# The last projection of a hybrid encoder layer: ten token tiles in one group, seven block products per column pair

## The chip, the cores and the metric

The kernel runs on one core of one Trainium2 chip. The metric is the device time of one execution in microseconds. The kernel before took 2684.31 us in the median of three runs (2681.81 to 2684.42).

Names of the engines: PE is the tensor engine (PEld its weight loads), DVE the vector engine, ACT the scalar engine, POOL the GpSimd engine, SP the engine whose queue issues all DMAs of this kernel. SBUF is the working memory, PSUM the accumulators in eight banks of 512 columns each.

## The reference

One layer of an encoder with two kinds of heads, computed for 1024 and 256 tokens, in fp32:

```python
hn = rmsnorm(x, norm_w)
proj = jnp.einsum('btd,dp->btp', hn, w_in)
# group A: neighbourhood attention, times a SiLU gate       -> att, 1024 wide
# group B: bidirectional mLSTM, norm, two gates             -> mem, 1024 wide
mixed = jnp.concatenate([att, mem], axis=-1)
return x + jnp.einsum('btm,md->btd', mixed, w_out)
# and last: y = rmsnorm(y, final_norm_w)
```

The change touches only the last lines: a product of 1280 tokens by 2048 by 2048 columns, plus the residual `x`, and the norm of each row.

## The kernel before

All token counts are together 1280 = 10 tiles of 128. The layer runs in three stages. Stage A projects the first 768 tokens; it already uses seven block products for a 2x2 block matrix (lines 314 to 383). Then the remaining 512 tokens are projected in pairs of 128 columns (`proj_pair`, line 488), interleaved with attention and mLSTM, which leave their result in DRAM as 16 blocks `mixT[k]` of 128 features by 1280 tokens. At the end of that, `late_gate` (line 530) projects the gates of the last 512 tokens, multiplies them into `mixT` and stores it back: first for features 1024 to 2047 (line 1168), then for features 0 to 1023 (line 1182). Last comes the output projection.

Every fp32 matrix product is made of three passes. An operand is split into a high part (a cast to fp32r on ACT, line 151) and a low part (source minus high part, a subtraction on DVE, line 152); high x high, high x low and low x high are accumulated. A matmul of the last stage has a 128x128 piece of `mixT` as the stationary operand and 512 columns of the output weights as the moving one, so a bank holds 128 tokens by 512 columns.

The output projection before (lines 1171 to 1244) goes over three groups of token tiles, `OG`: four, four and two. For a group all 16 blocks of `mixT` are loaded and split into the buffers that held the inputs of the projections before (`x_pair`, line 137). For each of four column blocks of 512, eight weight pieces of 512 KB are loaded and split (`w_split`, line 477), and for each block `k` the tiles of the group are multiplied with it. The last four blocks are held until the end, and then run tile by tile, so that the banks are finished one after the other. Each finished bank is read by DVE, which adds the residual (line 1240), ACT squares the result and sums it (line 1241), and POOL multiplies it with the norm weight (line 1242). After the fourth column block `finish` (line 1189) takes the row's reciprocal root mean square and scales and stores the row.

The order on each engine is chosen when the kernel is built, by a scheduler that follows the program's order and the buffers; at run time each engine keeps to that order. All loads and stores go through the one queue of SP, in order.

Of the kernel before, what the change touches and what calls it, by code (L numbers as in the profile page):

```python
# [13 lines left out]
P = 128  # L14
D = 2048
# [23 lines left out]
def kernel(  # L39
# [26 lines left out]
    def bank(tag, name):  # L66
        return ps.tile([P, 512], F32, tag=tag, name=name, bufs=3 if tag == "pr" else 5)
# [398 lines left out]
    def po(name):  # L466
        return wb.tile([P, 520], F32, tag="po", name=name, bufs=NPO)
# [6 lines left out]
        DM.dma_start(dst, src)  # L474
        return raw

    def w_split(raw, lo_, hi_, name, keep=False):
        n = hi_ - lo_
        if keep:
            t = yp.tile([P, 2, 512], F32R, tag="wk", name=f"ws_{name}", bufs=4)  # L480
        else:
            t = wb.tile([P, 2, 544], F32R, tag="wsp", name=f"ws_{name}", bufs=4)
        split(t[:, 0, :n], t[:, 1, :n], raw[:, lo_:hi_])
        return t

# [637 lines left out]
        for J in range(nc_):  # L1123
            yield out_unit(J)

    ahead = {}

    class LazyX:
        def __init__(self):
            self.t = {}  # L1130
# [37 lines left out]
    for ch in range(0, 8, 2):  # L1168
        late_gate(OT0 + ch, 8 + ch, X)

    OG = ((0, 4), (4, 4), (8, 2))

    def mix_raw(g, k):
        t0, n = OG[g]
        raw = po(f"mraw{g}_{k}")[:, : n * P]
        DM.dma_start(raw, mixT[k][:, t0 * P : (t0 + n) * P])
        return raw

    for h in range(0, NA_H, 2):
        if h == NA_H - 2:  # L1180
            ahead = {k: mix_raw(0, k) for k in range(2)}
        late_gate(GT0 + h, h, X)
    att_ctx.close()

    yp = ctx.enter_context(tc.tile_pool(name="yp", bufs=2))
    fnb = yp.tile([P, D], F32, tag="fnb", name="fnb", bufs=1)
    DM.dma_start(fnb, fnw.partition_broadcast(P))

    def finish(t, yt, ss):
        rs = yp.tile([P, 1], F32, tag="rs", name=f"rs{t}", bufs=4)  # L1190
        V.tensor_reduce(rs, ss, axis=mybir.AxisListType.X, op=ALU.add)
        rsqrt_mean(rs, rs, 1, float(D))
        w_ = 512 if t == TT // P - 1 else 1024
        for i in range(D // w_):
            cs = slice(i * w_, i * w_ + w_)
            if i % 2:
                S.mul(yt[:, cs], yt[:, cs], rs)
            else:
                V.tensor_scalar(yt[:, cs], yt[:, cs], rs, None, op0=ALU.mult)
            DM.dma_start(y[t * P : (t + 1) * P, cs], yt[:, cs])  # L1200

    for g, (t0, n) in enumerate(OG):
        mh, ml_ = [None] * KT, [None] * KT
        for k in range(KT):
            raw = ahead[k] if g == 0 and k in ahead else mix_raw(g, k)
            mh[k], ml_[k] = x_pair(k, f"m{g}_{k}")
            split(mh[k][:, : n * P], ml_[k][:, : n * P], raw)
        yt = [yp.tile([P, D], F32, tag="y", name=f"y{g}_{t}", bufs=5) for t in range(n)]
        ss = [yp.tile([P, 4], F32, tag="ss", name=f"ss{g}_{t}", bufs=8) for t in range(n)]

        def out_mm(o, tt, k, t, first, last):
            for i, (wi, xi) in enumerate(((1, 0), (0, 0), (0, 1))[:: 1 if tt % 2 else -1]):
                PE.matmul(  # L1213
                    o, (mh[k], ml_[k])[xi][:, tt * P : (tt + 1) * P], t[:, wi, :512],
                    start=first and i == 0, stop=last and i == 2,
                )

        for nb in range(4):
            held = []
            n_hold = 8 if (g, nb) == (2, 3) else 4  # L1220
            banks = [bank("pr" if nb % 2 and i < 3 else "a", f"po{g}_{nb}_{i}") for i in range(n)]
            for kp in range(0, KT, 2):
                nm = f"o{g}_{nb}_{kp}"
                raw = yp.tile([P, 1024], F32, tag="wr", name=f"wr_{nm}", bufs=4)
                DM.dma_start(raw, w_o[nb, :, kp * 512 : kp * 512 + 1024])
                for q in range(2):
                    k = kp + q
                    t = w_split(raw, q * 512, q * 512 + 512, f"{nm}_{q}", KT - n_hold <= kp < KT - 4)
                    if kp >= KT - n_hold:
                        held.append((k, t))  # L1230
                        continue
                    for tt in range(n):
                        out_mm(banks[tt], tt, k, t, k == 0, False)
            for tt in range(n):
                for i, (k, t) in enumerate(held):
                    out_mm(banks[tt], tt, k, t, False, i == n_hold - 1)
                cs = slice(nb * 512, nb * 512 + 512)
                xr = yp.tile([P, 512], F32, tag="xr", name=f"xr{g}_{nb}_{tt}", bufs=4)
                DM.dma_start(xr, xtok[(t0 + tt) * P : (t0 + tt + 1) * P, cs])
                V.tensor_tensor(yt[tt][:, cs], banks[tt], xr, op=ALU.add)  # L1240
                S.activation(xr, yt[tt][:, cs], AF.Square, accum_out=ss[tt][:, nb : nb + 1])  # L1241
                G.tensor_tensor(yt[tt][:, cs], yt[tt][:, cs], fnb[:, cs], op=ALU.mult)  # L1242
                if nb == 3:
                    finish(t0 + tt, yt[tt], ss[tt])


def _layout(inputs):
# [84 lines left out]
```

## Time and profile before

| | |
|---|---|
| median of three runs | 2684.31 us |
| span of the profiled execution | 2680.8 us |
| PE, busy | 2631.7 us |
| DVE, busy | 1797.0 us |
| ACT, busy | 1307.0 us |
| POOL, busy | 617.9 us |
| read from and written to device memory | 322.28 and 66.13 MB |
| granted clock of PE, mean | 0.997 |

The profile is of one execution. Its span runs from the first to the last instruction; the time of a run also holds what lies around it. A row of the groups of instructions names the line, the engine, the operation, the tile written and the tiles read, shapes and count; behind the bar stand the busy time in us and the mean of one instruction in ns, and after the second bar how long the engine was idle ahead of these instructions and what ended the wait. Line 151 and 152 are helpers, so one looks at the tile's name: `ws_o` are split weights of the last projection, `m_` split mix blocks, `po` its banks.

### The profile page before, as it was taken

The numbers are of one execution on the slowest core, as the hardware profiler recorded it, in microseconds if no ns is written. First come the engines' busy times: TensorE is split into PE (matmuls) and PEld (weight loads), VectorE is DVE, ScalarE is ACT, GpSimd is POOL, SyncE is SP. The second block draws the span as 40 slices with busy tenths as digits, with TensorE's granted clock in tenths as the row PEclk, the third lists the DMA queues.
The fourth block names the chain that finished last, engine by engine and source line by source line (L and its number), as shares of the span: only waits on it lengthen the run. The fifth ranks groups of instructions, "written<-read, shape, count | busy, mean of one in ns | idle before, by whom it ended". The sixth has DMA issues, their size and how long they took to land.

```text
span 2680.8 us, 42790 instructions
## 1 busy us (share of the span) xinstructions
PE 2631.7 (98%) x14710; PEld 2407.5 (90%) x14710; DVE 1797.0 (67%) x3645; ACT 1307.0 (49%) x2995; POOL 617.9 (23%) x897
## 2 busy tenths in 40 slices
PE   8999999999999999999999999999999999999998
PEld 8899999999999999988888898998888888878876
DVE  7867878788877878773676677586577444353455
ACT  7534444444444444533665666665665223242344
POOL 0434445444444444200110110100010000020121
PEclk9999999999999999999999999999999999999999
DMA  6423333332323233535555555655654545354465
GB/s 207 154 73 124 109 112 114 103 95 95 107 77 113 95 100 97 177 111 162 168 176 172 188 167 169 209 163 170 207 158 148 189 141 198 112 197 152 135 222 171
DMA packets 206435, 391.24 MB, mean 146 GB/s; under 512 B 25952, under 2 KB 117256, under 8 KB 206088
## 3 DMA queue, kind: packets, MB, share of 16 engines
q1 hardware_dynamic: 206216, 388.49, 45.3%
q8 instruction: 116, 1.90, 0.3%
q14 instruction: 103, 0.84, 0.1%
HBM read 322.28 MB, written 66.13 MB: 145 GB/s over the span
## 4 chain that ended last, share of the span: by engine, by line
PE 51%; DMA 4%; DVE 3%; ACT 1%; issue 1%; SPq 0%; POOL 0%; ACTq 0%; POOLq 0%; DVEq 0%
PE pc L500 20%; PE po L1213 16%; PE pv L581 5%; PE A54b L188 1%; PE A52b L188 1%; DMA wr<-in_w_in_dram 1%; PE nap_0s L618 1%; PE nap_1s L618 1%; DMA nap_0vr<-vD 0%; DMA mlp_0zr<-pT 0%; DMA wr_o<-in_w_o_dram 0%; PE nap_1o L744 0%; PE nap_0t L635 0%; PE nap_1t L635 0%; PE nap_0o L744 0%
## 5 line engine op out<-in xcount | busy, mean ns | idle before, releaser
L152 DVE TENSOR_TENSOR ws_o<-wr_o,ws_o 128x512 fp32r<-128x512 f32 x192 | 148.2, 783 | 150.4 <-ACT ws_o L151 148.3
L152 DVE TENSOR_TENSOR ws<-wr,ws 128x512 fp32r<-128x512 f32 x224 | 153.2, 694 | 127.1 <-ACT ws L151 125.7
L151 ACT CAST ws<-wr 128x512 fp32r<-128x512 f32 x224 | 136.9, 619 | 176.1 <-PE pc L500 133.7
L151 ACT CAST ws_o<-wr_o 128x512 fp32r<-128x512 f32 x192 | 116.5, 618 | 173.4 <-PE po L1213 146.9
L1242 POOL TENSOR_TENSOR y<-y,fnb 128x512 f32<-128x512 f32 x40 | 58.1, 1463 | 538.1 <-ACT xr L1241 517.1
L1240 DVE TENSOR_TENSOR y<-po,xr 128x512 f32<-128x512 f32 x40 | 27.5, 689 | 51.0 <-PE po L1213 51.0
L1241 ACT ACTIVATE xr<-y 128x512 f32<-128x512 f32 x40 | 25.2, 629 | 65.6 <-DVE y L1240 65.6
L165 DVE TENSOR_TENSOR pco<-pc,rstdb 128x512 f32<-128x512 f32 x48 | 32.9, 687 | 35.7 <-PE pc L500 34.1
L152 DVE TENSOR_TENSOR wsv<-wr_v,wsv 128x512 fp32r<-128x512 f32 x64 | 44.0, 693 | 18.8 <-ACT wsv L151 15.3
L102 POOL TENSOR_SCALAR mls_0r<-mls_0r 128x2 f32<-128x2 f32 x4 | 1.2, 289 | 234.6 <-ACT mls_0jk L1090 234.6
L151 ACT CAST wsv<-wr_v 128x512 fp32r<-128x512 f32 x64 | 38.8, 616 | 31.6 <-PE pc L500 19.3
L274 DVE SCALAR_TENSOR_TENSOR pcv<-pco,cw_sb,pcv 128x516 f32<-128x516 f32 x64 | 46.6, 748 | 0.0
L500 PE MATMUL pc<-x_0h,ws 128*128 128x512 f32 x112 | 36.0, 401 | 0.9 <-DVE pco L165 0.9
L188 PE MATMUL fb<-xg,fw 128*128 128x384 f32 x192 | 35.1, 336 | 1.7 <-ACT xg L158 1.7
L500 PE MATMUL pc<-x_2h,ws 128*128 128x512 f32 x112 | 35.4, 399 | 0.0
L188 PEld LDWEIGHTS fb<-xg,fw 128*128 128x128 f32 x192 | 33.3, 188 | 2.2 <-ACT xg L158 2.2
L500 PE MATMUL pc<-x_8h,ws 128*128 128x512 f32 x112 | 34.6, 396 | 0.0
L500 PE MATMUL pc<-x_1h,ws 128*128 128x512 f32 x112 | 34.4, 395 | 0.0
L188 PE MATMUL fb<-xb,fw 128*128 128x384 f32 x96 | 23.2, 355 | 11.0 <-ACT xb L158 11.0
L500 PE MATMUL pc<-x_9h,ws 128*128 128x512 f32 x112 | 33.7, 397 | 0.0
L500 PE MATMUL pc<-x_5h,ws 128*128 128x512 f32 x112 | 33.1, 397 | 0.0
L500 PE MATMUL pc<-x_4h,ws 128*128 128x512 f32 x112 | 33.1, 397 | 0.0
(1734 smaller groups left out, 8767.0 us busy)
## 6 DMA issues: line engine op xcount, KB each, us to landing
wr<-in_w_in_dram SPq DMA_DIRECT2D x112, 512.0 KB
wr_o<-in_w_o_dram SPq DMA_DIRECT2D x96, 512.0 KB
wr_v<-in_w_in_dram SPq DMA_DIRECT2D x32, 512.0 KB
xq<-in_xtok_dram SPq DMA_DIRECT2D x20, 512.0 KB
xr<-in_xtok_dram SPq DMA_DIRECT2D x40, 256.0 KB
out_dram<-y SPq DMA_DIRECT2D x18, 512.0 KB
mraw<-mx SPq DMA_DIRECT2D x32, 256.0 KB
xr<-in_xT_dram SPq DMA_DIRECT2D x16, 384.0 KB
```

The lines of the kernel that those rows point to most:

```text
L151: S.copy(hi, src)
L152: V.tensor_tensor(lo, src, f(hi), op=ALU.subtract)
L165: V.tensor_tensor(o, src, rb, op=ALU.mult)
L188: PE.matmul(o, w(a_), x(b_), start=first and m == 0, stop=last and m == 2)
L274: V.scalar_tensor_tensor(dst[:, a:n], src[:, a + j - pad : n + j - pad], cw_sb[:, ct, j : j + 1], dst[:, a:n], op0=ALU.mult, op1=ALU.add,)
L500: PE.matmul(pb[j], t[j][:, wi, c : c + P], xs[xi], start=first and m == 0, stop=last and m == 2,)
L581: PE.matmul(outs[tt], xs[:, tt * P : (tt + 1) * P], t[:, wi, q * w : (q + 1) * w], start=first and m == 0 and (gates or tt % 2 == 0), stop ...
L618: PE.matmul(b[:, :nkeys], qs(a_), ks(b_), start=i == 0, stop=i == 2)
L1213: PE.matmul(o, (mh[k], ml_[k])[xi][:, tt * P : (tt + 1) * P], t[:, wi, :512], start=first and i == 0, stop=last and i == 2,)
L1240: V.tensor_tensor(yt[tt][:, cs], banks[tt], xr, op=ALU.add)
L1241: S.activation(xr, yt[tt][:, cs], AF.Square, accum_out=ss[tt][:, nb : nb + 1])
L1242: G.tensor_tensor(yt[tt][:, cs], yt[tt][:, cs], fnb[:, cs], op=ALU.mult)
```

## The change

The output projection is one group of all ten tiles. The mix matrix is cut into 2 x 2 blocks: features 0 to 1023 and 1024 to 2047 (`kh`), and tokens 0 to 639 and 640 to 1279 (`th`, five tiles each). In the code `a` and `d` are the blocks of the first tokens (low and high features), `e` and `c` those of the last tokens. The weights are taken for a pair `p` of two column blocks, again as 2 x 2 blocks (`b11`, `b12`, `b21`, `b22`). The four result blocks of a pair are then sums of seven products instead of eight. Written with the numbers of the code, in the order in which they run: product 2 = d x b21; 5 = (e + c) x (b12 - b11); 1 = a x b11; 6 = (e + c - a) x T2 with T2 = b22 - b12 + b11; 7 = (c - e') x (b22 - b12); 4 = c x (T2 - b21); 3 = (d - e') x b22, where e' is the block e after e + c - a was put in its place. For the second pair product 2 comes last, and is marked as the tail, whose blocks are all split ahead and which runs tile by tile.

A product has eight blocks `kk` of 128 features. For each, ACT and DVE split a mix piece of 128x640 into a buffer `mo` (four of them) and a weight piece of 128x512 into a buffer `wsp` (four). Sums of mix blocks are made by DVE, in place or in a buffer `ms` (two), sums of weight blocks by POOL. The last two blocks are held (`HOLD`), and then each tile's bank is finished and read.

The result blocks are accumulators `Y` in SBUF, in the buffers of the earlier inputs (`xslot`). They are loaded with the residual `xtok` (`y_init`), and each finished bank is added to one or two of them by DVE (`y_add`); the banks of products 1, 6 and 7 are the same, accumulated further. Finished blocks are squared by ACT and, except for two of the second pair, multiplied with the norm weight by POOL (`y_done`); those of the first pair are stored to a scratch in DRAM (`yD`) and loaded again when the row is scaled (`finish`). Weights that are used as they are come in pieces of 512 KB (`w_pure`, three buffers), those that are summed in pieces of 256 KB (`w_block`, in the six buffers `po`). All 32 mix pieces are loaded before, as soon as the memory of the attention is free.

The core of the diff, new lines:

```python
    def operands(p, i, kk):
        n0, n1 = 2 * p, 2 * p + 1
        a, c, d, e = Aa[kk], Ac[kk], Ad[kk], Ae[kk]
        if i == 2:
            return d, w_pure(1, n0, kk, nm)
        if i == 5:
            b12, b11 = w_block(0, n1, kk, nm + "a"), w_block(0, n0, kk, nm + "b")
            t = T2[kk] = xslot(20 + kk, f"T2_{nm}")
            DM.dma_start(t, w_o[n1, :, (8 + kk) * 512 : (9 + kk) * 512])
            G.tensor_tensor(b12, b12, b11, op=ALU.subtract)
            G.tensor_tensor(t, t, b12, op=ALU.subtract)
            if p:
                return m_sum(e, a, ALU.add, f"ms{nm}"), b12
            V.tensor_tensor(e, e, c, op=ALU.add)
            return e, b12
        if i == 1:
            return a, w_pure(0, n0, kk, nm)
        if i == 6:
            if p == 0:
                V.tensor_tensor(e, e, a, op=ALU.subtract)
            return e, T2[kk]
        if i == 7:
            b22, b12 = w_block(1, n1, kk, nm + "a"), w_block(0, n1, kk, nm + "b")
            G.tensor_tensor(b22, b22, b12, op=ALU.subtract)
            return m_sum(c, e, ALU.subtract, f"ms{nm}"), b22
        if i == 4:
            b21 = w_block(1, n0, kk, nm)
            G.tensor_tensor(b21, T2[kk], b21, op=ALU.subtract)
            return c, b21
        return m_sum(d, e, ALU.subtract, f"ms{nm}"), w_pure(1, n1, kk, nm)

    def y_add(p, q, tt, bk, op=ALU.add):
        V.tensor_tensor(Y[p, q, tt], Y[p, q, tt], bk, op=op)

    def y_done(p, q, tt):
...
        S.activation(jk, Y[p, q, tt], AF.Square, accum_out=ss[t][:, c : c + 1])
        if p == 0 or q in (1, 3):
            G.tensor_tensor(Y[p, q, tt], Y[p, q, tt], fnb[c], op=ALU.mult)
        if p == 0:
            DM.dma_start(yD[t][:, nh * 512 : (nh + 1) * 512], Y[p, q, tt])

    def finish(th, tt):
...
        for i in (2, 0, 3, 1):
            if i == 2:
                V.scalar_tensor_tensor(out[i], out[i], rs, fnb[i], op0=ALU.mult, op1=ALU.mult)
            elif i < 2:
                S.mul(out[i], out[i], rs)
            else:
                V.tensor_scalar(out[i], out[i], rs, None, op0=ALU.mult)
            DM.dma_start(y[t * P : (t + 1) * P, i * 512 : (i + 1) * 512], out[i])

    HOLD = 2

    def product(p, i, bk, first, each):
        held = []
        tail = (p, i) == (1, 2)
...
        for kk in range(8):
            ms, wsrc = operands(p, i, kk)
...
                t = mp.tile([P, 2, TH], F32R, tag="mo", name=f"mo{nm}", bufs=4)
                m = [t[:, z] for z in range(2)]
            split(*m, ms)
...
                t = wb.tile([P, 2, 544], F32R, tag="wsp", name=f"wo_{nm}", bufs=4)
                w = [t[:, z, :512] for z in range(2)]
            split(*w, wsrc)
            if tail or kk >= 8 - HOLD:
                held.append((kk, m, w))
                continue
            for tt in range(NT):
                mms(tt, kk, m, w, False)
        for tt in range(NT):
            for kk, m, w in held:
                mms(tt, kk, m, w, kk == 7)
            each(tt)
...
    for p in range(2):
...
        if p == 0:
            c11_second()
        y_init(p, 1)
        y_init(p, 3)
        bk = p_banks(p, 1)
        product(p, 5, bk, True, reads(bk, (1, ALU.add), (3, ALU.add)))
        if p:
            y_init(p, 0)
        ch = p_banks(p, 2)
        product(p, 1, ch, True, reads(ch, (0, ALU.add), done=0 if p == 0 else None))
        y_init(p, 2)
        product(p, 6, ch, False, reads(ch, (1, ALU.add)))
        product(p, 7, ch, False, reads(ch, (2, ALU.add), (3, ALU.add), done=3))
        bk = p_banks(p, 3)
        product(p, 4, bk, True, reads(bk, (2, SUB), done=2, fin=1))
        bk = p_banks(p, 4)
        product(p, 3, bk, True, reads(bk, (1, ALU.add), done=1))
        if p:
            c11_second()
```

`c11_second` runs product 2 into result block 0. The old loop over `OG` with `mix_raw`, its early loads `ahead`, and the kept weight buffers of `w_split` are taken out. Nothing ahead of the output projection is changed.

More of the change, by code (lines that the diff above doesn't have):

```diff
@@ L1124, in ml_units @@
             yield out_unit(J)
-    ahead = {}
     class LazyX:
@@ L1202 @@
[L1202 to L1212, printed above, removed]
+    mp = ctx.enter_context(tc.tile_pool(name="mp", bufs=1))
```

157 lines of the change are left out of this document (102 added, 55 removed).

## The prediction

> **What bounds the kernel now.** I read the page first, then the stretches of the final projection (line 1213), then who waited for whom there.
>
> ```profile
> span 2680.8 us, 42790 instructions
> PE 2631.7 (98%) x14710; PEld 2407.5 (90%) x14710; DVE 1797.0 (67%) x3645; ACT 1307.0 (49%) x2995; POOL 617.9 (23%) x897
> ...
> PEclk9999999999999999999999999999999999999999
> ```
>
> PE is the bound of the whole kernel, at full granted clock. The chain of waits between 2150 us and the end shows where the final projection begins, and the table of stretches how densely PE works in it (columns: length, busy us and count of PE, PEld, DVE, ACT, POOL, clock, DMA share, GB/s):
>
> ```profile
> 2149.77 70.39 PE pc L500 x303
> 2220.16 173.16 PE po L1213 x749
> ```
>
> ```profile
> 2220.10:2401.00 180.90, 180.90 (x784) 146.89 (x783) 82.22 (x117) 66.87 (x129) 22.96 (x18) 1.00 0.50 162
> 2401.00:2410.00 9.00, 8.20 (x36) 6.37 (x35) 8.02 (x12) 5.82 (x10) 4.46 (x7) 1.00 0.83 285
> 2410.00:2575.00 165.00, 165.00 (x715) 133.91 (x714) 62.19 (x88) 48.56 (x101) 18.82 (x15) 1.00 0.45 144
> 2575.00:2600.00 25.00, 20.48 (x84) 14.92 (x83) 16.26 (x24) 13.80 (x25) 8.70 (x10) 1.00 0.84 303
> 2600.00:2671.00 71.00, 70.90 (x309) 57.47 (x307) 43.61 (x60) 35.75 (x65) 12.03 (x9) 1.00 0.58 187
> 2671.00:2680.80 9.80, 0.00 (x0) 0.00 (x0) 1.67 (x4) 2.08 (x5) 2.00 (x3) 0.61 0.56 214
> ```
>
> ```profile
> PE po L1213 <- DVE ws_o L152: 3.2, 4, 1.5
> PE po L1213 <- ACT ws_o L151: 2.1, 1, 2.1
> ```
>
> The projection lasts from 2220.1 to 2671.0, 450.9 us, and PE idles 5.3 us of it, where a new token group starts (2401, 2575 to 2600). The code issues 16 contraction blocks x 4 column blocks x 10 token tiles x 3 passes = 1920 matmuls, so one costs (450.9 - 5.3) / 1920 = 0.232 us. DVE, ACT and the DMA queues have slack there; what PE has to do sets this stage.
>
> **What is removed: a fact of counting.** The new stage has 2 column pairs x 7 products x 8 blocks x 5 tiles x 3 passes = 1680 matmuls, and the compiled order of PE holds that number, of the same shape (128x128 stationary, 512 moving) with the same pass order. 240 x 0.232 = 55.7 us go. One product of 120 matmuls then costs 27.85 us of PE. The group changes go too, and with them their 5.3 us.
>
> **What is added, off PE.** All operands that are sums must be made. By engine, from these rows of the final stage (mean ns is the second number after the bar):
>
> ```profile
> L152 DVE TENSOR_TENSOR ws_o<-wr_o,ws_o 128x512 fp32r<-128x512 f32 x190 | 146.9, 784 | 146.2 <-ACT ws_o L151 144.1 <-DMA xr<-in_xtok_dram 0.7
> L151 ACT CAST ws_o<-wr_o 128x512 fp32r<-128x512 f32 x190 | 115.2, 618 | 169.1 <-PE po L1213 146.9 <-DMA wr_o<-in_w_o_dram 10.7 <-ACT xr L1241 4.7
> L1240 DVE TENSOR_TENSOR y<-po,xr 128x512 f32<-128x512 f32 x40 | 27.5, 689 | 51.0 <-PE po L1213 51.0
> L152 DVE TENSOR_TENSOR m_9l<-mraw,m_9h 128x512 fp32r<-128x512 f32 x2 | 1.4, 689 | 1.5 <-ACT m_9h L151 1.5
> L152 DVE TENSOR_TENSOR m_9l<-mraw,m_9h 128x256 fp32r<-128x256 f32 x1 | 0.4, 426 | 1.6 <-ACT m_9h L151 1.6
> L1242 POOL TENSOR_TENSOR y<-y,fnb x40: 1262/1462/1753, 2261.3 to 2672.5; 128x512 f32<-128x512 f32 x40
> ```
>
> An undisturbed 512-wide DVE operation is 0.69 us and a 256-wide one 0.43, so the 640-wide ones of the new code are about 0.69 + 0.13 = 0.82. A POOL operation of 512 is 1.26 us at least, 1.46 in the middle. ACT has two casts for each block, 0.62 and about 0.62 x 640/512 = 0.77, with PE taking 15 x 0.232 = 3.48 us for that block: never the bound. DMA: weights fall from 96 x 512 KB to 144 blocks of 256 KB, the new scratch copy of half the output adds 20 x 256 KB each way; the sum stays near the old one, and the heaviest product asks for 24 blocks of 256 KB, 6.3 MB in 27.85 us, 226 GB/s, where the table above shows 303 in one stretch. Loading the residual into what becomes the accumulators replaces a load of the same size.
>
> **Where DVE and POOL meet.** The mean of 784 ns against 689 has a cause which the order in time shows (start, length, engine):
>
> ```profile
> 2261.76 0.69 DVE L1240 TENSOR_TENSOR y<-po,xr 128x512 f32<-128x512 f32 x1 [0.70 <-PE po L1213]
> 2263.16 2.91 DVE L152 TENSOR_TENSOR ws_o<-wr_o,ws_o 128x512 fp32r<-128x512 f32 x2 [0.71 <-DMA xr<-in_xtok_dram]
> ...
> 2586.18 3.32 DVE L152 TENSOR_TENSOR ws_o<-wr_o,ws_o 128x512 fp32r<-128x512 f32 x5
> ...
> 2606.71 3.72 DVE L152 TENSOR_TENSOR ws_o<-wr_o,ws_o 128x512 fp32r<-128x512 f32 x3 [0.28 <-ACT ws_o L151]
> ```
>
> ```profile
> 2261.25 4.27 POOL L1242 TENSOR_TENSOR y<-y,fnb 128x512 f32<-128x512 f32 x3 [199.06 <-ACT xr L1241]
> ...
> 2605.96 3.33 POOL L1242 TENSOR_TENSOR y<-y,fnb 128x512 f32<-128x512 f32 x2 [20.48 <-DMA wr_o<-in_w_o_dram]
> ```
>
> Alone, five subtractions take 3.32 us. Beside POOL, two take 2.91 and three take 3.72: each POOL operation is served in turn with them. The add from the accumulators (2261.76) is not slowed, although POOL is in the middle of its work. So subtractions and sums of two operands in SBUF and POOL's operations add up, and adds from PSUM do not.
>
> The Trainium skill says the same, and more strictly (page "SBUF — State Buffer", section "Who interferes with whom"): a DVE instruction with two SBUF inputs contends with a POOL instruction that reads SBUF, and the second one blocks fully. By that rule every such pair is serial, which would give the full excess of the third rival below wherever no buffer lets the work run ahead; the rows agree for the operations they show.
>
> Now the products one by one. PE may run one when its blocks are split; 4 operand buffers let DVE be two blocks ahead at the change of product, and the last two blocks are held to the end, so block 7 is due 6/8 x 27.85 = 20.9 us after a product starts. Product 5 is the heavy one: two POOL subtractions and three DVE operations for each block.
>
> First column pair: in the compiled order of DVE, 28 instructions stand from the first add of product 2 (possible when its first tile is complete, 22.2 us into product 2) to the last weight split of product 5: 5 adds, 7 weight splits (12 x 0.69 = 8.3), and 6 mix splits, 7 subtractions for product 6, 2 sums, 1 difference (16 x 0.82 = 13.1), 21.4 us. POOL has 12 operations in the same stretch, 15.1 us. The time available is 27.85 - 22.2 + 20.9 = 26.5 us. Fully overlapped: no wait. Serial but for the 3.5 us of adds: 21.4 + 15.1 - 3.5 - 26.5 = 6.5 us late. The rows speak for serial; back-to-back DVE spacing (3.32 / 5 = 0.66) takes a little off: I take 6.
>
> Second pair: 24 DVE instructions (12 x 0.69 + 12 x 0.82 = 18.1) and 10 POOL operations (12.6), since five blocks of product 5's weights stand ahead of it in POOL's order: 18.1 + 12.6 - 3.5 - 26.5 = 0.7. I take 1, with 0 to 7 (five output multiplications more, 6.3).
>
> Product 7 has one POOL operation for each block: 18.1 + 8 x 1.26 - 3.5 = 24.7 < 26.5, no wait; products 1, 2, 3, 4 and 6 have fewer.
>
> The other changes of product wait for single operands as the old changes of column block did. There 11 changes cost 5.3 us; 13 new ones by the same rate 6.3, between 0 and 2.1 (the longest wait above) each.
>
> **Entry and end.** All 32 mix blocks are now loaded (0.33 MB each) among the weight loads of the last gate projections, on the one SP queue. The old kernel put 2 MB of output weights and 1 MB of norm weights there. The first product reads only blocks whose last gate was finished long before. I take 0, up to 5 us. At the end:
>
> ```profile
> 2672.46 1.26 POOL L1242 TENSOR_TENSOR y<-y,fnb 128x512 f32<-128x512 f32 x1 [2.63 <-ACT xr L1241]
> ...
> 2674.66 0.88 DVE L1199 TENSOR_SCALAR y<-y,rs 128x512 f32<-128x512 f32 x2 [2.09 <-POOL rs L103]
> ```
>
> the last multiplication by the norm weight leaves POOL for a fused DVE operation (0.69 instead of 0.44): about 1.0 us off the 9.8 us tail.
>
> **Sum.** Against the profiled span: 2680.8 - 55.7 - 5.3 + 6 + 1 + 6.3 - 1.0 = 2632.1. The median of the runs, 2684.3, lies 3.5 above the span, which I keep: 2635.6, so 2636 us.
>
> **Rivals.** (a) DVE and POOL together become the bound of the whole stage, with work banked freely between products. DVE: 112 mix splits and 56 sums x 0.82, 112 weight splits and 90 adds x 0.69, closing work 10 x 1.3, together 290 us; POOL 94 x 1.46 = 137. In full series 427.5 us in place of 450.9: 2684.3 - 23.4 - 1 = 2660. For it: the 0.66 to 1.46 rows. Against it: adds overlap, and this earlier stretch:
>
> ```profile
> 250.00:1200.00 950.00, 944.89 (x5493) 928.51 (x5493) 747.82 (x1403) 434.18 (x1021) 395.60 (x487) 1.00 0.34 108
> ```
>
> There DVE is busy 79% and POOL 42% of the time with the same kind of product, waits for each other included, and PE still works 99.5%.
>
> (b) The SP queue blocks. Stores and loads stand in one order; in the compiled order the loads for product 5's later blocks stand behind a weight load for product 1 that can go only after product 2's last split (its buffer comes free after block 3, 4 x 3.48 = 13.9 us into the product), and behind the last gate's two stores, which wait for DVE behind a split that needs block 4's buffer (5 x 3.48 = 17.4 us, and some operations more). If each of the later blocks comes one block time late, four times 3.48: 14 us more, 2650.
>
> (c) Slower: nothing can be banked, since the order on each engine is fixed and operand buffers hold two blocks ahead. Then each product costs the larger of PE and DVE + POOL in series. At 1.46: product 5 has 18.6 + 6.9 + 23.4, with 6.6 for product 6's subtractions (first pair) or 7.3 of output multiplications (second) 55.5 and 56.2; product 7 37.2; product 4 34.6; product 3 29.4 and 28.7. Over 27.85 that is 27.6 + 28.3 + 2 x 9.3 + 2 x 6.7 + 1.5 + 0.8 = 90.2 us: 2684.3 - 55.7 - 5.3 + 90.2 - 1 = 2713. It decides from 62 us of excess on. Against it: the add at 2261.76, and five blocks of POOL work ahead in the second pair.
>
> **How the numbers follow.** Forecast, 2624 to 2648: 0.60. (a) 0.18. (b) 0.10. (c) in its costly part 0.09; near no change 0.03. What can be told from no change here is about 0.2%. Low end: only 3 us of waits in the sum, 2625, with a little for the entry: 2622. High end: past (a), 2668. Faster 0.88, same 0.03, slower 0.09.
>
> **What would show it.** Right: 1680 matmuls of 0.232 us; PE idle in the final stage 10 to 20 us, most of it in the first product 5, released by DVE; weight splits there near 1.2 us mean, adds from accumulators at 0.69; POOL operations at 1.5. Wrong: PE idle spread over products 7, 4 and 3 too (a, c); PE or ACT released by a DMA (b); a later start of the first product (entry); a slower matmul, which nothing here leads me to expect.

## The result and the profile after

The changed kernel takes 2636.83 us in the median of four runs (2631.05 to 2639.76), the kernel before, beside it on the same chip, 2683.57 us. The ratio is 0.9825, with a 95% interval of 0.981 to 0.984. So it is faster by 47 us, 1.7%; the prediction said 2636.0 us, and its range of 2622 to 2668 holds the result.

The first lines of the page of the changed kernel, and the one row that a table of stretches gives for its whole output projection (length, then busy us and count of PE, PEld, DVE, ACT, POOL; clock, DMA share, GB/s):

```profile
span 2637.7 us, 42477 instructions
...
PE 2582.4 (98%) x14470; PEld 2364.1 (90%) x14470; DVE 1923.2 (73%) x3744; ACT 1309.2 (50%) x2988; POOL 709.1 (27%) x951
```

```profile
2222.20:2628.80 406.60, 394.02 (x1681) 314.91 (x1679) 333.15 (x393) 173.47 (x316) 158.97 (x112) 1.00 0.49 162
```

PE has 240 instructions less than before, DVE 99 and POOL 54 more. The projection lasts 406.5 us in place of 450.9. Its matmuls in the order of time, with the pauses of PE in brackets and what ended them:

```profile
2222.20 32.78 PE L1300 MATMUL po<-wo,mo 128*128 128x512 f32 x141
2257.55 3.74 PE L1300 MATMUL po<-wo,mo 128*128 128x512 f32 x15 [2.57 <-DVE wo L152]
...
2266.78 6.25 PE L1300 MATMUL po<-wo,mo 128*128 128x512 f32 x26 [1.60 <-DVE wo L152]
...
2279.21 12.79 PE L1300 MATMUL po<-wo,mo 128*128 128x512 f32 x54 [0.95 <-DVE wo L152]
2292.45 118.53 PE L1300 MATMUL po<-wo,mo 128*128 128x512 f32 x512 [0.45 <-DVE mo L152]
2411.68 3.27 PE L1300 MATMUL po<-wo,mo 128*128 128x512 f32 x13 [0.71 <-DVE wo L152]
...
2440.52 0.71 PE L1300 MATMUL po<-wo,mo 128*128 128x512 f32 x2 [0.39 <-DVE mo L152]
2442.11 3.27 PE L1300 MATMUL po<-wo,mo 128*128 128x512 f32 x13 [0.89 <-DVE wo L152]
...
2453.80 101.90 PE L1300 MATMUL po<-wo,mo 128*128 128x512 f32 x432 [0.88 <-DVE wo L152]
2556.42 51.81 PE L1300 MATMUL po<-wo,mo 128*128 128x512 f32 x223 [0.72 <-DVE wo L152]
...
2625.85 2.88 PE L1300 MATMUL po<-wt,mo 128*128 128x512 f32 x12
```

How to read it: a product has 120 matmuls, so the first pause, after 141, falls into the second product in order, the first product 5. In the row at 2292.45, 512 matmuls go from the first start to the last end in 118.53 us; less the 0.39 us that one takes by itself, that is 118.14 / 511 = 0.2312 us from start to start. The prediction's row of before with 749 matmuls in 173.16 us gives 0.2310 by the same working. So 1680 matmuls need 388.4 us, the projection took 2628.7 - 2222.2 = 406.5, and 18.1 us are lost. PE's idle time by the profile is 12.5 us: each pause costs 0.2 to 0.3 us more than it shows, and matmuls at a lower clock count as busy (1.7 us, see the last section). Counted from the first start of a product to the first start of the next, less 120 x 0.2312, the losses are 7.2 us in the first product 5, 7.5 in the second, 0.7 in the first product 1, 1.8 in the first product 3 and 1.2 in the second product 4. In the other nine products nothing is lost (0.1 us either way).

Who ended PE's waits:

```profile
PE po L1300 <- DVE wo L152: 9.9, 10, 2.6
PE po L1300 <- DVE mo L152: 2.6, 5, 0.7
```

All of it is DVE's splits, of weights (`wo`) and of mix blocks (`mo`), and none a DMA. Three groups of operations (before the bar the shapes and the count; behind it busy us and mean ns) answer to the costs that the prediction gave them:

```profile
L1250 DVE TENSOR_TENSOR y<-y,po 128x512 f32<-128x512 f32 x90 | 57.6, 678 | 12.8 <-PE po L1300 12.8
...
L1265 POOL TENSOR_TENSOR y<-y,fnb 128x512 f32<-128x512 f32 x30 | 48.1, 1621 | 36.3 <-ACT jk L1263 35.8
L1214 DVE TENSOR_TENSOR ms<-mb,mb 128x640 f32<-128x640 f32 x40 | 45.1, 1127 | 0.0
```

The adds from the accumulators keep their 0.68 us; the sums of two mix blocks are at 1.13 in place of 0.82, and POOL's multiplications at 1.62 against 1.46 before. What lies under the means is seen in the second product 5, DVE first and then POOL:

```profile
2434.92 1.78 DVE L152 TENSOR_TENSOR wo<-wb_3a,wo 128x512 fp32r<-128x512 f32 x1
2436.62 1.91 DVE L1214 TENSOR_TENSOR ms<-mb,mb 128x640 f32<-128x640 f32 x1
2438.45 1.92 DVE L152 TENSOR_TENSOR mo<-ms,mo 128x640 fp32r<-128x640 f32 x1
...
2447.34 0.81 DVE L1214 TENSOR_TENSOR ms<-mb,mb 128x640 f32<-128x640 f32 x1
```

```profile
2427.61 1.30 POOL L1227 TENSOR_TENSOR wb_5a<-wb_5a,wb_5b 128x512 f32<-128x512 f32 x1 [12.99 <-DMA wb_5b<-in_w_o_dram]
...
2434.27 3.57 POOL L1265 TENSOR_TENSOR y<-y,fnb 128x512 f32<-128x512 f32 x2
2437.81 1.88 POOL L1228 TENSOR_TENSOR T<-T,wb_6a 128x512 f32<-128x512 f32 x1
2439.65 3.55 POOL L1265 TENSOR_TENSOR y<-y,fnb 128x512 f32<-128x512 f32 x2
```

A DVE operation of two SBUF operands takes 0.68 (512 columns) or 0.81 us (640) alone and 1.78 or 1.91 while POOL has work: every POOL operation costs DVE 1.1 us. POOL had stood idle for 13.0 us for the load of a weight block, and then did its last sums and five norm multiplications (`y<-y,fnb`) just when PE was waiting for DVE.

### The profile page after: what moved, and what is told of

It reads as the page before. It is cut to its first block, busy times and chain, and to the rows that moved or that the text cites. A ratio compares the mean times of both kernels' runs of the same rounds, so it can differ in the third digit from the quotient of the medians.

```text
span 2637.7 us, 42477 instructions
## 1 busy us (share of the span) xinstructions
PE 2582.4 (98%) x14470; PEld 2364.1 (90%) x14470; DVE 1923.2 (73%) x3744; ACT 1309.2 (50%) x2988; POOL 709.1 (27%) x951
## 4 chain that ended last, share of the span: by engine, by line
PE 45%; DVE 8%; DMA 4%; ACT 2%; issue 1%; SPq 1%; POOL 0%; ACTq 0%; POOLq 0%; DVEq 0%
PE pc L497 21%; PE po L1300 10%; PE pv L578 4%; DVE mo L152 2%; DVE wo L152 1%; PE A54b L188 1%; DMA wr<-in_w_in_dram 1%; DVE ms L1214 1%; PE A52b L188 1%; DVE y L1250 1%; PE nap_0s L615 1%; PE nap_1s L615 1%; DMA nap_0vr<-vD 0%; DVE mb L1237 0%; PE nap_2o L741 0%
## 5 line engine op out<-in xcount | busy, mean ns | idle before, releaser
L1300 PE MATMUL po<-wo,mo 128*128 128x512 f32 x1620 | 381.0, 395 | 12.5 <-DVE wo L152 9.9
L1300 PEld LDWEIGHTS po<-wo,mo 128*128 128x128 f32 x1620 | 303.8, 188 | 88.9 <-DVE wo L152 14.9
L151 ACT CAST mo<-mb 128x640 fp32r<-128x640 f32 x72 | 51.8, 725 | 108.1 <-PE po L1300 92.4
L152 DVE TENSOR_TENSOR mo<-mb,mo 128x640 fp32r<-128x640 f32 x72 | 72.9, 1023 | 38.8 <-ACT mo L151 38.8
L1250 DVE TENSOR_TENSOR y<-y,po 128x512 f32<-128x512 f32 x90 | 57.6, 678 | 12.8 <-PE po L1300 12.8
L151 ACT CAST mo<-ms 128x640 fp32r<-128x640 f32 x40 | 29.0, 725 | 70.8 <-PE po L1300 32.5
L152 DVE TENSOR_TENSOR mo<-ms,mo 128x640 fp32r<-128x640 f32 x40 | 48.5, 1214 | 13.2 <-ACT mo L151 13.2
L1265 POOL TENSOR_TENSOR y<-y,fnb 128x512 f32<-128x512 f32 x30 | 48.1, 1621 | 36.3 <-ACT jk L1263 35.8
L165 DVE TENSOR_TENSOR pco<-pc,rstdb 128x512 f32<-128x512 f32 x48 | 32.8, 686 | 27.8 <-PE pc L497 26.1
L1214 DVE TENSOR_TENSOR ms<-mb,mb 128x640 f32<-128x640 f32 x40 | 45.1, 1127 | 0.0
L1263 ACT ACTIVATE jk<-y 128x512 f32<-128x512 f32 x40 | 25.2, 631 | 39.7 <-DVE y L1250 38.2
```

The costliest lines, as they stand in the source:

```text
L151: S.copy(hi, src)
L152: V.tensor_tensor(lo, src, f(hi), op=ALU.subtract)
L165: V.tensor_tensor(o, src, rb, op=ALU.mult)
L1214: V.tensor_tensor(t, x, y_, op=op)
L1250: V.tensor_tensor(Y[p, q, tt], Y[p, q, tt], bk, op=op)
L1265: G.tensor_tensor(Y[p, q, tt], Y[p, q, tt], fnb[c], op=ALU.mult)
```

## The experiments

The theory was that of the prediction: DVE's two-operand work and POOL's work are served in turn, and what is due before product 5's last block decides. Rivals were that DVE is overbooked by its own work (rival 1), that the loads come late (rival 2), and that POOL's own rate sets when the weight sums are there (rival 3). The stage is the output projection from the start of its first matmul to the end of its last; lost is the stage less 388.4 us, matmuls at a lower clock included. All the code ahead of it is the same in these kernels, and yet it began between 2214.2 and 2224.3 us, so single profiles are compared by the stage.

| kernel | median us (runs) | ratio to before, 95% | stage us | lost us |
|---|---|---|---|---|
| as changed | 2636.8 (4) | 0.981 to 0.984 | 406.5 | 18.1 |
| all weight sums on DVE | 2625.7 (4) | 0.9767 to 0.9796 | 395.3 | 6.9 |
| first pair's norm multiplications late | 2634.6 (4) | 0.9798 to 0.9833 | 404.2 | 15.8 |
| without T2's subtraction | 2621.3 (4) | 0.9751 to 0.978 | 391.2 | 2.8 |
| e - a late | 2631.4 (4) | 0.979 to 0.9819 | 399.3 | 10.9 |
| T2 set to zero | 2620.4 (1) | | 390.7 | 2.3 |
| POOL's sum in product 7 twice | 2645.3 (1) | | 417.8 | 29.4 |
| four blocks held | 2665.2 (1) | | 430.1 | 41.7 |
| weight sums on DVE and e - a late | 2626.8 (5) | 0.9771 to 0.9797 | 394.6 | 6.2 |
| product 5's weight sums on DVE | 2626.5 (5) | 0.9773 to 0.9803 | 397.0 | 8.6 |
| weight sums on DVE, five multiplications late | 2625.0 (4) | 0.9762 to 0.9799 | 394.0 | 5.6 |

**All weight sums on DVE.**

```diff
-            G.tensor_tensor(b12, b12, b11, op=ALU.subtract)
-            G.tensor_tensor(t, t, b12, op=ALU.subtract)
+            V.tensor_tensor(b12, b12, b11, op=ALU.subtract)
+            V.tensor_tensor(t, t, b12, op=ALU.subtract)
...
-            G.tensor_tensor(b22, b22, b12, op=ALU.subtract)
+            V.tensor_tensor(b22, b22, b12, op=ALU.subtract)
...
-            G.tensor_tensor(b21, T2[kk], b21, op=ALU.subtract)
+            V.tensor_tensor(b21, T2[kk], b21, op=ALU.subtract)
```

> Edit: the 64 sums and differences of weight blocks (products 5, 7, 4 of both pairs) go from POOL to DVE; POOL keeps the norm multiplications. Theory (DVE operations with two SBUF operands and POOL operations are served in turn): a POOL operation holds DVE up by about 1.1 us (DVE operations of 640 columns took 1.90 instead of 0.81 us beside POOL), and costs about 0.68 us as a DVE operation, so DVE gets no worse: PE's gap in the first product 5 stays between 3 and 9 us, total 2628 to 2640 us. Rival 1 (DVE is overbooked by its own work, POOL has no part in it): 16 more operations of 0.68 us in each product 5 make it 11 us later there, about 2655 to 2660 us. Rival 2 (the loads of the weight blocks come late): gaps unchanged, about 2637 us, released by DMA through DVE.

The row of its whole stage:

```profile
2221.00:2616.30 395.30, 389.86 (x1681) 314.62 (x1679) 315.77 (x455) 173.20 (x316) 53.41 (x48) 1.00 0.50 166
```

DVE has 64 operations more, of 0.68 us each, 43.5 us in all, and yet it is busy for 17.4 us less (315.8 against 333.2). The 64 operations had cost it (17.4 + 43.5) / 64 = 0.95 us each while they were POOL's, more than doing them itself. PE's loss falls by 11.2 us, the time by 11.1. Rival 1 forecast 18 us or more the other way, rival 2 no change, and both fall. The theory's own numbers were too timid: the first product 5 loses 2.0 us, not 3 to 9. The largest part of what is left lies in the first product 3, 2.6 us where the kernel as changed loses 1.8, and DVE's operations there are stretched to 1.8 to 1.9 us beside POOL's norm multiplications. The 2.0 us of the second product 5 stand beside POOL too; its DVE in the order of time:

```profile
2426.53 1.78 DVE L1228 TENSOR_TENSOR T<-T,wb_6a 128x512 f32<-128x512 f32 x1
2428.24 1.75 DVE L152 TENSOR_TENSOR wo<-wb_2a,wo 128x512 fp32r<-128x512 f32 x1
```

its POOL at the same time,

```profile
2426.39 3.05 POOL L1265 TENSOR_TENSOR y<-y,fnb 128x512 f32<-128x512 f32 x2 [0.46 <-ACT jk L1263]
```

and its PE:

```profile
2430.04 70.13 PE L1300 MATMUL po<-wo,mo 128*128 128x512 f32 x302 [1.74 <-DVE wo L152]
```

The split at 2428.24 took 1.75 us beside two norm multiplications, and PE stood 1.74 us until it was done.

**The first pair's norm multiplications late.** They go into the closing step, where DVE does them together with the row scale.

```diff
-        if p == 0 or q in (1, 3):
+        if p and q in (1, 3):
...
-            if i == 2:
+            if i < 3:
                 V.scalar_tensor_tensor(out[i], out[i], rs, fnb[i], op0=ALU.mult, op1=ALU.mult)
-            elif i < 2:
-                S.mul(out[i], out[i], rs)
             else:
-                V.tensor_scalar(out[i], out[i], rs, None, op0=ALU.mult)
+                S.mul(out[i], out[i], rs)
```

> Edit: the 20 norm multiplications of the first pair are taken from POOL; the closing step multiplies those blocks by row scale and norm weight in one DVE operation. Theory (in turn): five POOL operations of 1.7 us leave the second pair's product 5, each worth about 1.1 us to DVE, so PE's idle time there falls from 5.5 to between 0 and 2 us and the gap between matmul starts from about 9 to 2 to 4; the first product 5 is unchanged; total 2630 to 2633 us. Rival 1 (DVE's own work): no change in either product 5, 2637 us. Rival 2 (late load of a weight block, for which POOL stood idle for 13 us in the second pair): that wait stays and PE's gap with it, 2635 to 2638 us. In every case the closing steps of ten tiles get 20 DVE operations of two SBUF operands, which may add up to 1.5 us after the last matmul.

PE's matmuls in the order of time:

```profile
2299.77 276.91 PE L1298 MATMUL po<-wo,mo 128*128 128x512 f32 x1198
...
2580.41 17.66 PE L1298 MATMUL po<-wo,mo 128*128 128x512 f32 x75 [2.35 <-DVE mo L152]
2599.16 1.89 PE L1298 MATMUL po<-wo,mo 128*128 128x512 f32 x7 [1.09 <-ACT wo L151]
```

The new DVE operations, a row of its groups of instructions:

```profile
L1285 DVE SCALAR_TENSOR_TENSOR yr<-yr,rs,fnb 128x512 f32<-128x512 f32 x20 | 14.1, 745 | 0.0
```

and POOL's sum of block 5 in the order of time:

```profile
2426.78 1.43 POOL L1227 TENSOR_TENSOR wb_5a<-wb_5a,wb_5b 128x512 f32<-128x512 f32 x1 [20.89 <-DMA wb_5b<-in_w_o_dram]
```

From 2300 to 2577 us, through the whole second product 5, PE has no pause (1198 matmuls in 276.9 us are 0.231 each). POOL waits 20.9 us for the load of block 5, which lands at 2426.8 us, as late as in the kernel as changed (2427.6), and it costs nothing: rival 2 falls, and so does rival 1 for this product. The first product 5 loses 9.3 us; 1.7 of them are a stretch of 3.4 us at half clock behind its last pause, and the other 7.6 are about as before (7.2), as forecast. The mechanism holds, but the gain is given back in the last two products, where the 20 new DVE operations stand: 3.1 us are lost in product 3, with DVE at their work, and 3.7 in product 2. In product 2 a load has a part: ACT's casts wait 6.0 us for it, where the kernel as changed has 0.4 us,

```profile
2590.41 1.14 ACT L151 CAST wt<-wr_wp 128x512 fp32r<-128x512 f32 x2 [5.96 <-DMA wr_wp<-in_w_o_dram]
```

and it was issued at 2582.9 us, behind the stores of the closing step in SP's queue. That these stores came late because of the new DVE operations is not shown. The total is 2 us lower, which the intervals do not tell from no change.

**Without T2's subtraction.**

```diff
             G.tensor_tensor(b12, b12, b11, op=ALU.subtract)
-            G.tensor_tensor(t, t, b12, op=ALU.subtract)
```

> Edit: the second POOL operation of each block in product 5 (b22 - b12 + b11, an operand of products 6 and 4) is left out, so those two products are computed with b22 in its place. Theory (in turn): 16 POOL operations fewer, eight in each product 5, of which five or more stand inside the stretch that decides, worth 1.1 us each: both gaps fall from about 9 to between 0 and 4 us, total 2622 to 2629 us. Rival 1 (DVE's own work): nothing changes for DVE, 2637 us. Rival 2 (late loads): the gaps stay, 2634 to 2638 us. Rival 3 (POOL's own rate sets when the weight sums are ready, whatever it does to DVE): the same fall as in the theory, but with DVE waiting for POOL ahead of it in the kernel as changed.

PE in the order of time, from the first product 5 on:

```profile
2252.84 3.73 PE L1299 MATMUL po<-wo,mo 128*128 128x512 f32 x15 [0.81 <-DVE wo L152]
2256.73 280.68 PE L1299 MATMUL po<-wo,mo 128*128 128x512 f32 x1211 [0.16 <-DVE wo L152]
```

Here 1.5 us are lost in the first product 5 and none in the second. DVE has the same instructions as in the kernel as changed, so rival 1 falls again; this run alone does not tell the theory from rival 3. The trace of the kernel as changed does: by rival 3 DVE would wait there for POOL's sums. In the first product 5 DVE waits for nothing, and in the second this is the only wait, in us, times and the longest:

```profile
DVE mo L152 <- ACT mo L151: 1.2, 2, 0.8
```

**T2 set to zero,** by a POOL operation that writes and reads nothing.

```diff
-            G.tensor_tensor(t, t, b12, op=ALU.subtract)
+            G.memset(t, 0.0)
```

> Edit: POOL's second operation of each block in product 5 writes zeros into its tile and reads nothing, so products 6 and 4 are computed without their weight block. Theory, strict form (only a POOL operation that reads SBUF takes turns with DVE): DVE's operations of 640 and 512 columns beside the zeroing stay at 0.81 and 0.68 us, the gaps in both products 5 fall to 0 to 4 us as without the operation (2.6 us of gaps in all there), total 2619 to 2626 us. Theory, wide form (any POOL operation takes turns): they take 1.9 and 1.75 us beside it, gaps as in the kernel as changed, 17.7 us in all, total 2633 to 2638 us. Rival 3 (POOL's own rate): gaps by the zeroing's length alone, DVE operations not slowed.

POOL in the order of time, where the first zeroings stand,

```profile
2223.68 0.53 POOL L1228 MEMSET T<- 128x512 f32 x1 [0.15 <-DMA T<-in_w_o_dram]
2224.36 0.53 POOL L1228 MEMSET T<- 128x512 f32 x1 [0.15 <-DMA T<-in_w_o_dram]
```

and DVE at the same time:

```profile
2223.32 0.83 DVE L152 TENSOR_TENSOR mo<-mb,mo 128x640 fp32r<-128x640 f32 x1
2224.06 0.69 DVE L152 TENSOR_TENSOR wo<-wp,wo 128x512 fp32r<-128x512 f32 x1
```

The splits keep 0.83 and 0.69 us with a zeroing in the middle of each, and all 16 zeroings take 0.52 to 0.53 us. So the strict form holds for these zeroings: a POOL operation that reads nothing does not take turns with DVE. The Trainium skill says so (page "SBUF — State Buffer", section "Who interferes with whom"), and the trace agrees. The zeroing does not wait for the first sum either, so it moved ahead in time, and that too keeps it out of DVE's way.

**e - a late.** A factor that is always 1, made from product 5's last bank, binds the differences to the end of product 5.

```diff
-                V.tensor_tensor(e, e, a, op=ALU.subtract)
+                V.scalar_tensor_tensor(
+                    e, e, one[0], a, op0=ALU.mult, op1=ALU.subtract
+                )
...
+        if p == 0:
+            one.append(mp.tile([P, 1], F32, tag="one", name="one"))
+            V.tensor_scalar(one[0], bk[4][:, 0:1], 0.0, 1.0, op0=ALU.mult, op1=ALU.add)
```

> Edit: the first pair's differences e - a for product 6 (eight DVE operations, 0.81 us alone, 1.9 beside POOL) are bound to the last bank of product 5, so none of them stands among product 5's splits. Theory (in turn) and rival 1 (DVE's own work) alike: seven operations of 0.81 us leave the stretch, PE's gap in the first product 5 falls from 8.5 by 5 to 6 us, the second is unchanged; but the eight now stand in a row behind the five pairs of adds, 6.6 us of DVE, and product 1 may wait for its third block by 0 to 5 us; total 2632 to 2637 us. Rival 2 (late loads): the gap stays at 8 to 9 us, 2637 us or more.

PE in the order of time:

```profile
2253.05 30.05 PE L1303 MATMUL po<-wo,mo 128*128 128x512 f32 x129 [0.52 <-DVE wo L152]
...
2292.74 7.62 PE L1303 MATMUL po<-wo,mo 128*128 128x512 f32 x32 [1.88 <-DVE mo L152]
```

The first product 5 loses 0.8 us in place of 7.2, product 1 now 2.9. So it was DVE's list there that was too long, not a load; the theory and rival 1 forecast this alike. The second product 5 still loses 6.8, 1.7 of them at half clock. Both changes that helped the first product 5 together (all weight sums on DVE as well):

> Edit: both changes that shortened the first product 5: the 64 sums and differences of weight blocks on DVE, and the first pair's e - a bound to the last bank of product 5. Theory (DVE's two-operand work and POOL's work take turns; what is due before a product's last block decides): with the sums on DVE the first product 5 keeps a gap of 1.9 us, which falls to 0 to 1; product 1 gets eight subtractions in a row, as in the run with the late differences alone, where that cost 2.1 us (there with POOL beside them, here without: 0 to 2). Total 2623 to 2627 us against 2625.7 with the sums on DVE alone. Rival (DVE's own work is now the bound wherever it is put): nothing gained, the gap moves to product 1 whole, 2626 to 2630 us.

The first product 5 loses nothing any more, product 1 loses 1.4, and the stage is 0.7 us shorter than with the sums alone. The time cannot tell the two kernels apart, 2626.8 and 2625.7 us, nor the theory from its rival here: 2626.8 lies in both ranges.

**POOL's sum in product 7 twice.**

```diff
+            dm = mp.tile([P, 512], F32, tag="dm", name=f"dm{nm}")
+            G.tensor_tensor(dm, b22, b12, op=ALU.subtract)
             G.tensor_tensor(b22, b22, b12, op=ALU.subtract)
```

> Edit: in product 7 each block gets a second POOL subtraction of the same two weight blocks, whose result nobody uses. Theory (in turn), by the sum that the prediction made for product 7 (24.7 us of work against 26.5): eight operations of 1.1 to 1.3 us more make 33.5 to 35, so 7 to 8.6 us late in each of the two products 7, together 14 to 17 us: 2651 to 2654 us, PE released by DVE there; product 5 as before. Rival (POOL's work overlaps DVE's, or DVE has slack from other products): under 4 us in all, 2636 to 2641 us, and POOL's busy time up by 21 to 26 us.

The row of the whole stage:

```profile
2216.80:2634.60 417.80, 398.52 (x1681) 316.21 (x1679) 352.72 (x392) 173.19 (x316) 190.09 (x128) 0.99 0.48 157
```

PE in the order of time, and below it POOL:

```profile
2334.63 74.09 PE L1302 MATMUL po<-wo,mo 128*128 128x512 f32 x319
2409.04 0.71 PE L1302 MATMUL po<-wo,mo 128*128 128x512 f32 x2 [0.33 <-DVE mo L152]
...
2454.58 0.75 PE L1302 MATMUL po<-wo,mo 128*128 128x512 f32 x2 [3.21 <-DVE mo L152]
```

```profile
2333.72 1.30 POOL L1242 TENSOR_TENSOR dm<-wb_5a,wb_5b 128x512 f32<-128x512 f32 x1 [17.98 <-DMA wb_5b<-in_w_o_dram]
```

DVE is busy for 19.6 us more (352.7 against 333.2) with the same instructions: 1.2 us for each of the 16 added POOL operations. That is the theory's price, and rival 3 has no place for it. But both forecasts of the time miss. Neither product 7 loses anything, the first runs inside the 319 matmuls from 2334.63 on; 11.3 us more are lost in other products, most in the second product 5 (12.0 in place of 7.5), the second product 4 (3.6 in place of 1.2) and the first products 1 and 5; 3.4 of the 11.3 are matmuls at half clock (see the last section). For product 7 the prediction's sum of all eight blocks was too strict: POOL had done blocks 0 to 4 when it began to wait for block 5's load, 18 us before 2333.7, while product 7 itself starts at about 2339.

**Four blocks held,** `HOLD = 4` in place of 2.

> Edit: the last four blocks of each product are held in place of two, so no operand buffer is free for the next product's blocks until the last tile runs. Theory (the changes of product cost nothing because two blocks are split ahead): each of the 13 changes costs 0.5 us (the rate of the old kernel's group and column changes, which held four) to 2 us (one cast and one subtraction and their hand-overs), and the two products 5 lose the two blocks of lead, 2 to 7 us each: total 2645 to 2677 us. Rival (the changes are free by the order of work alone): 2637 to 2641 us.

PE in the order of time:

```profile
2263.68 6.32 PE L1300 MATMUL po<-wo,mo 128*128 128x512 f32 x15 [4.89 <-DVE wo L152]
...
2566.01 1.17 PE L1300 MATMUL po<-wo,mo 128*128 128x512 f32 x4 [0.63 <-ACT wo L151]
...
2597.49 14.76 PE L1300 MATMUL po<-wo,mo 128*128 128x512 f32 x57 [2.61 <-DVE mo L152]
```

Now there are pauses at the changes of product: 2566.01 is where the second product 4 starts, 2597.49 where the second product 3 does. The first product 5 loses 13.8 us. All in all 23.5 us more are lost, about 10 of them at changes of product and 6.8 at half clock. Seven of the thirteen changes now have a pause of 0.5 us or more and the other six have 0.2 us or none: at those seven it is the two blocks split ahead that make the change free in the kernel as changed.

**Only product 5's weight sums on DVE** (the first two lines of the first diff of this section).

> Edit: only product 5's own two operations per block (b12 - b11, and T2) go from POOL to DVE, 32 in all; the sums of products 7 and 4 stay on POOL. Theory (in turn, and only what is due before a product's last block counts): product 5 is where PE waited, so moving these 32 is enough: gaps there as with all 64 moved (about 2 us in each product 5), products 7 and 4 without a gap as before, total 2624 to 2629 us. Rival 1 (DVE needs relief over the whole stage, a debt that is carried from product to product): half of the gain, 2630 to 2633 us, since each of the 32 operations left on POOL still takes 1.1 us of DVE's time, and DVE stays fuller than with all 64 moved.

The row of its whole stage:

```profile
2218.80:2615.80 397.00, 390.11 (x1681) 314.72 (x1679) 319.00 (x424) 173.69 (x316) 112.51 (x80) 1.00 0.50 165
```

The products 5 lose 2.0 and 1.9 us, the same as with all 64 moved. Products 7 lose nothing; the first product 4 now loses 2.1, which the theory did not have, and the first product 3 loses 2.8. Moving half of the operations brings 9.5 of the 11.2 us of stage, and a time inside the theory's range and below that of rival 1.

**All weight sums on DVE, five norm multiplications late:** those of the first pair's product 3.

```diff
-        if p == 0 or q in (1, 3):
+        if (p, q) != (0, 1) and (p == 0 or q in (1, 3)):
...
-            if i == 2:
+            if i == 2 or (th, i) == (0, 1):
                 V.scalar_tensor_tensor(out[i], out[i], rs, fnb[i], op0=ALU.mult, op1=ALU.mult)
-            elif i < 2:
+            elif i < 2 or (th, i) == (0, 3):
                 S.mul(out[i], out[i], rs)
```

> Edit: all 64 weight-block operations on DVE, and the five norm multiplications that POOL did at the end of the first pair's product 3 are taken from it; the closing step of the first five tiles does them on DVE, after the last product has begun. Theory (in turn): with the sums on DVE the trace has these five POOL operations exactly where DVE is late for the second product 5 (splits of 1.75 and 1.4 us beside them, a gap of 2.1 us); without them that gap is 0 to 0.5, total 2622 to 2626 us against 2625.7. Rival 1 (DVE's own work): the gap of 2.1 stays, and the five operations of 0.75 us more lengthen the end by up to 0.8 us: 2625 to 2628 us.

PE in the order of time, about the second product 5:

```profile
2396.24 39.09 PE L1300 MATMUL po<-wo,mo 128*128 128x512 f32 x168 [0.48 <-DVE mo L152]
2435.51 64.67 PE L1300 MATMUL po<-wo,mo 128*128 128x512 f32 x278 [0.17 <-DVE mo L152]
```

The pause of 1.74 us in the second product 5 is gone, 0.17 is left; counted from start to start it loses 0.4 us in place of 2.0. This kernel's stage of 394.0 us and its median of 2625.0 us are the lowest of all kernels that keep T2's subtraction; but the four kernels with weight sums on DVE lie within 2 us, and their intervals overlap. What is shown is that each of them is faster than the kernel as changed (every upper end, 0.9803 at most, lies below 0.981).

## Why the prediction came out right

Term by term, against the span of before, losses counted from start to start:

| step | predicted us | measured us |
|---|---|---|
| 240 matmuls less | -55.7 | -55.5 (240 x 0.2312) |
| old changes of group | -5.3 | -7.0 (450.9 - 1920 x 0.2312) |
| late in the first product 5 | +6 | +7.2 |
| late in the second product 5 | +1 (0 to 7) | +7.5 |
| 13 other changes of product (measured: all else that is lost) | +6.3 | +3.4 |
| entry | 0 (up to 5) | +2.1 |
| end | -1.0 | -0.8 (9.0 against 9.8) |
| span | 2632.1 | 2637.7 |

**What held.** The matmul count and their cost; that PE still sets the stage; that the first product 5 is late by DVE and POOL in series, and by about how much; that adds from accumulators are not slowed. For the first product 5 the working itself holds: the same 28 DVE operations run without a pause from 2246.4 to 2279.2 us, 32.8 us, where the step had 21.4 + 15.1 - 3.5 = 33.0 (15 POOL operations begin beside them, where it had counted 12). The eight weight splits there have a mean of 1.22 us, as forecast (four of 0.68 us, four of 1.75 to 1.78). PE idles 12.5 us, inside the forecast 10 to 20. One of the signs did not come: 5.8 of these 12.5 us lie in the first product 5, which is not most of them.

**Second product 5: mis-sized.** The step took the value 0.7 "since five blocks of product 5's weights stand ahead of it in POOL's order", and left "five output multiplications more" for the upper end. Of the 7.5 us, 1.7 are a lower clock; the other 5.8 lie near the upper end. Five blocks were ahead, as the step had it: POOL had done their sums by 2405.7 us. But then it stood idle for 13.0 us, and the last three blocks' sums and five multiplications fell together with DVE's last splits: 13 POOL operations begin between the first add and the end of the last weight split, not 10. The run with the first pair's norm multiplications late shows what counted: without them the product loses nothing, though the load is as late. It took all 20 away; that the last five count by themselves is shown only for what the weight sums on DVE had left (2.0 us, then 0.4).

**The 13 other changes: a term without ground.** The step has them wait "as the old changes of column block did", at 5.3 us for 11 changes. But those 5.3 us are the ones that the prediction had put down to the new token groups and taken off in the term before. Its own table shows it: from 2220.10 to 2401.00 and from 2410.00 to 2575.00, with three changes of column block in each, PE is busy throughout. Counted from start to start, 7.1 us of the old kernel lie behind its two changes of group (1.1 and 6.0) and none at its nine changes of column block. In the new kernel the 13 changes cost nothing either; the 3.4 us lie inside products 1, 3 and 4, where DVE's splits are late. That a charge of 6.3 came near a loss of 3.4 is luck.

**Entry.** The stage began 2.1 us later than before. Kernels with the same code ahead began up to 8.0 us earlier and 2.1 later than that, so these profiles cannot say whether the change has a part in it.

**The sum.** The span came out 5.6 us longer than predicted, 3.3 of it from the losses (and the old ones), 2.1 from the entry, 0.2 from the end. The time fits to 1 us because the added 3.5 us from span to median was wrong as well: here the median lies 0.9 below the span of the profiled run, which took 2639.76 us and was the longest of four. Within the losses, 6.5 us too few in the second product 5 were met by 2.9 too many at the changes. So the mechanism of product 5 was right, the charge for the changes was not, and part of the closeness is chance.

**The rivals.** (a) asked for DVE and POOL in full series over the whole stage, 427 us; it took 406.5, with no loss in products 7. (b) forecast PE or ACT released by loads; no wait of PE ends at a DMA, and ACT's casts of this stage wait for loads for 0.4 us in all. Loads did come late for POOL (the 13.0 us), and count by what they push together. (c) forecast 9.3 us for each product 7 and 6.7 for each product 4; they lose nothing, and 0 and 1.2.

## What to carry to other kernels

A POOL operation with SBUF inputs is not free work beside DVE: here it cost DVE 1.0 to 1.2 us of its time, more than the 0.68 us that DVE needs to do the same, and giving 64 of them to DVE, which was busy 82% of the stage, saved 11 us. Count such operations where they fall in time, against what is due at the next product's last block, and look for what a late load pushes into the same stretch. Moving work in time only helps if the place that gets it has slack: the 20 multiplications moved to the end took there most of what they had saved, and the late differences took back 2.2 of the 6.4 us that they had saved in product 5.

## What the runs showed of the hardware

The granted clock of PE fell for a few microseconds after short pauses. The kernel as changed, in two stretches just behind the pauses of the second product 5 (length, PE busy and count, clock, DMA share, GB/s):

```profile
2455.00:2457.00 2.00, 2.00 (x6) 0.50 0.26 58
2457.00:2459.00 2.00, 2.00 (x8) 0.68 0.66 239
```

At 0.50 six matmuls lie in 2 us where full clock has nine, and 1.6 us are lost in these rows ((0.50 + 0.32) x 2), 1.7 in the whole stretch of 3.4 us from 2454.9. PE had not been idle for longer than 0.89 us at a time; in the first product 5 of the same run it was idle for 2.57 us, and the clock stayed at 1.00. The Trainium skill (page "TensorE: Matmul & The Clock Gate", section "Part 1: The HAM clock gate") has half rate follow an idle window of about 3.4 us that runs freely, which would make it a matter of how pauses fall into that window. The half rate and a length near 3.4 us agree with these rows; that the window must be idle as a whole does not, by the two pauses of 0.74 and 0.88 us at 2452 and 2454 with matmuls between them. With only product 5's sums moved to DVE no stretch of 2 us of the stage lies below 0.95; with four blocks held there are four such drops, one of them twice as long, and 8.5 us are lost by them in the same way.
